# Layer 1's SSD in a two-layer hybrid backbone: decay differences and order of the projections rewritten

## The chip, the cores and the metric

The kernel runs on one core of one Trainium2 chip. The metric is the device time of one execution in microseconds (us), median over runs. Besides the DMA queues the core has five engines that each work through their own instructions in program order: PE (TensorE), DVE (VectorE), ACT (ScalarE), POOL (GpSimd) and SP (SyncE, which here issues the DMAs).

## The reference

The reference is a two-layer backbone over 512 latent and 256 context tokens of width 1024. Layer 0 mixes with MLA attention beside an RWKV-7 scan, layer 1 with a Mamba-2 SSD scan beside windowed grouped attention with a sink; behind each mixer stands a convolutional FFN. The change touches layer 1's mixer alone:

```python
def ssd_scan(x, dt, a_log, bm, cm, h0):          # chunks of 128 tokens, 2 groups x 8 heads, 64 channels a head
    a_cum = jnp.cumsum(dtc * a, axis=2)
    seg = a_cum[:, :, :, None] - a_cum[:, :, None, :]
    decay_qk = jnp.exp(jnp.where(tri[:, :, None, None], seg, -jnp.inf))
    cb = jnp.einsum('bcqgn,bckgn->bcqkg', cc, bc)
    y_diag = jnp.einsum('bcqkgh,bckghp->bcqghp', cb[..., None] * decay_qk * dtc[:, :, None], xc)
    ...                                           # chunk states, carried from chunk to chunk: h_in
    y_off = jnp.einsum('bcqgn,bcghpn,bcqgh->bcqghp', cc, h_in, jnp.exp(a_cum))
    return y_diag + y_off, h_last

def ssd_bidirectional(f_ctx, f_lat, p):           # the same scan forwards and backwards, with decays of their own
    ...
def swa_latent(q, k, v, k_ctx, v_ctx, sink):      # per block of 128 queries: softmax over context and window, times v
    ...
def mixer_ssd_swa(h_ctx, h_lat, p, rope, need_ctx):
    z, xbc, dt, q, k, v = split_cols(h @ p['w_in'], CD_SPLITS)
    ...
    out_l = jnp.concatenate([gated_rms_norm(y_l, z_l, g), att_l], axis=-1) @ p['w_out']
```

## The kernel before

Every large product is `dense` (L367): 8 slices of the inner dimension, each in three passes, weights high part by activations high part, low by high, high by low. A weight tile of 128 output rows is loaded as `wraw` (512 KB), cast to `whi` by ACT (L327), and `wlo` is the rest, by DVE or POOL (L328). Over 768 tokens a tile is 24 pairs of matmuls of 512 and 256 columns, over the 512 latent ones 24 of 512. All matmuls go through `mm`, so they carry line 269. PSUM is shared by name: `acc` (two tiles of 1024 columns), `sd` (three of 512), `b1`.

The code is written stage by stage, and a list scheduler with a model of the engines fixes each engine's order before the run. It may put later independent instructions ahead of earlier ones; buffers and semaphores then hold an engine that comes too soon. On the chip an engine never passes a waiting instruction.

Layer 1's mixer runs in these steps:

1. `decays()` projects `dt`, cumulates the decays of 48 rows (two directions of 16 heads, padded), writes them to DRAM as `sp_ac`, and makes `acm` (the cumulated decay by token), `wgt`, `dec` and `dtm`.
2. B and C of both groups (`bf`, `cf`, `btm`), then, for the eight tiles of x, four to a group: `dense`, a convolution of five taps on ACT and DVE (`conv5`, L1247 and L1251), and six transposes to `xtm`.
3. For each group: ten chunk states (POOL `xw`, a product into `sd`, DVE `hn`: L1342 to L1352), four products `cb` of B and C, and then four latent chunks c, each in two directions d. For one (c, d):
 - a DMA spreads 8 heads' cumulated decay over all partitions, `E` of 128x8x128 (512 KB);
 - ACT takes its exponential as `G` (L1373), POOL multiplies it by C (L1374);
 - DVE subtracts the token's own decay from `E` and cuts it at 0, one instruction a head (L1376), ACT takes the exponential (L1378), DVE multiplies by `dtm` and the masked `cb`, one instruction a head (L1381).

 PE then forms for each head and direction two products into the same bank, `hn` by `G` and `xtm` by `E`: 32 products of 64 rows by 128 columns a chunk. DVE adds the bank to `ym` (L1393).
4. Keys, values and four query tiles, with rope and splits that go to DRAM (`sl_k`, `sl_q0` to `sl_q3`); the rope buffers take over the room of `xtm0`.
5. Eight tiles of z gate `ym`; then the windowed attention, block by block (`swa_block`): for each block of keys and each of the two key groups, scores into `ab`, an exponential `pt`, and the value product `o<-pt,vv`, 64 rows by 512 columns, each group into its own half of the partitions. Tiles of the output projection (`wo`) are worked in between.

In this order group 0's chunks come between x tiles of group 1, keys, values and queries, and group 1's chunks among the z tiles.

Of the kernel before, what the change touches and what calls it, by code (L numbers as in the profile page):

```python
# [212 lines left out]
def hybrid_kernel(ctx: ExitStack, tc: tile.TileContext, a, out):  # L213
# [1110 lines left out]
    open_pool("sw", "right")  # L1324
    seq = ([0, 1, 2, 3, 4, 5], [1, 0, 5, 4, 3, 2])
    for g in range(2):
        for j in range(4 * g, 4 * g + 4):
# [7 lines left out]
            token_major(xtm[j // 4][:, :, (j % 4) * P:(j % 4 + 1) * P], o)  # L1335
        hin = {}
        for d in range(2):
            hprev = None
            hs = slice(32 * d + 8 * g, 32 * d + 8 * g + 8)
            for i, c in enumerate(seq[d][:-1]):  # L1340
                xw = T("sw", [P, 512], "xw", 2)
                ptt(out=xw.rearrange(h3, x=64), in0=xtm[g][:, c].rearrange(h3, x=64),  # L1342
# [21 lines left out]
        for c in range(2, 6):
            ls = slice((c - 2) * P, (c - 1) * P)
            E, G = [], []
            for d in range(2):
# [2 lines left out]
                dma(e.rearrange("p h t -> p (h t)"),  # L1370
                    acd[c, h0:h0 + 8].rearrange("h t -> (h t)").unsqueeze(0).partition_broadcast(P))
# [1 line left out]
                act(gc, e, AF.Exp)  # L1373
                ptt(out=gc, in0=gc, in1=cf[g][:, ls].unsqueeze(1).to_broadcast([P, 8, P]), op=ALU.mult)  # L1374
                for h in range(8):
                    ts(out=e[:, h], in0=e[:, h], scalar1=acm[:, c, h0 + h:h0 + h + 1], scalar2=0.0, op0=ALU.subtract,  # L1376
                       op1=ALU.min)
                act(e, e, AF.Exp)  # L1378
                cb = cbs[c, d]
                for h in range(8):  # L1380
                    stt(out=e[:, h], in0=e[:, h], scalar=dtm[:, c, h0 + h:h0 + h + 1], in1=cb, op0=ALU.mult,  # L1381
                        op1=ALU.mult)
# [13 lines left out]
    rq = T("sx", [P, 6, 512], "xtm0")  # L1396
    ropc, rops = rq[:, 0], rq[:, 1]
# [118 lines left out]
    def swa_block(i, es):  # L1516
# [5 lines left out]
        for n, tb in enumerate(tbs):  # L1522
# [125 lines left out]
```

## Time and profile before

| | before |
|---|---|
| median of 3 runs | 2253.11 us (2247.74 to 2253.65) |
| the profiled execution | 2259.24 us, of which 2257.2 us from the first to the last instruction |
| mean granted PE clock | 0.955 |
| PE busy | 2066.3 us, 92% |
| DVE, ACT, POOL busy | 1393.8, 930.8 and 506.2 us |
| HBM traffic | 125 GB/s over the span |

Busy times are those of one profiled execution. In the rows that follow, `acc<-h,whi` means: written tile, then what was read, with buffer numbers left out; `xN` is a count of instructions. A PE product of two plain fp32 operands shows as two instructions, one of the split kind (fp32r) as one. Matmuls overlap, so that their durations add up to more than the time that passes; the distance from one start to the next is the better measure. The granted clock is a share of the full PE clock.

### The profile page before, as it was taken

Reading aid. Unit: us, or ns where it says so; the run is one execution under the profiler, and the core shown is the slowest. Engines: PE = TensorE matmul, PEld = TensorE weight load, DVE = VectorE, ACT = ScalarE, POOL = GpSimd, SP = SyncE. Lnnn points to the kernel's source line nnn. Section 1 sums busy time; section 2 is a strip of 40 time slices with the busy share of each in tenths; the row PEclk is TensorE's granted clock in tenths of the full one; section 3 lists DMA queues with packets and bytes.
Section 4 is the critical chain, followed back from the end, with each engine's and each line's share of the span. In section 5 each row is a group of like instructions: output and inputs, shape, how many; then the busy total and the mean of one; then the engine's idle time right before and its main releaser. Section 6 shows DMA issues by size and latency. Waiting matters only on the chain.

```text
span 2257.2 us, 33584 instructions
## 1 busy us (share of the span) xinstructions
PE 2066.3 (92%) x13360; PEld 1636.3 (72%) x13360; DVE 1393.8 (62%) x2157; ACT 930.8 (41%) x1437; POOL 506.2 (22%) x486
## 2 busy tenths in 40 slices
PE   5888989788998999999999999898878999999997
PEld 3666667576654878888888886776665667888886
DVE  5566865666877466456465554678984556554555
ACT  4445663532355253233132335644353345332434
POOL 0027686521233100000000014433631330000000
PEclk9989999698999999999999999998999999999998
DMA  8477777669521443333233333213426032323231
GB/s 300 121 202 197 192 204 192 213 175 294 168 96 54 152 140 114 102 103 119 87 115 101 103 112 117 90 47 117 133 85 159 28 126 71 94 89 98 84 117 61
DMA packets 183660, 292.00 MB, mean 129 GB/s; under 512 B 63616, under 2 KB 118944, under 8 KB 180432
## 3 DMA queue, kind: packets, MB, share of 16 engines
q1 hardware_dynamic: 183504, 289.86, 41.8%
q8 instruction: 105, 1.72, 0.3%
q14 instruction: 51, 0.42, 0.1%
HBM read 234.87 MB, written 47.33 MB: 125 GB/s over the span
## 4 chain that ended last, share of the span: by engine, by line
PE 64%; DVE 7%; ACT 5%; DMA 4%; issue 3%; POOL 1%; SPq 1%; DVEq 0%; ACTq 0%; POOLq 0%
PE acc L269 50%; PE sd L269 3%; PE b L269 3%; PE o L269 2%; PE ab L269 2%; PE wo L269 2%; DVE E L1376 2%; DMA E<-sp_ac 1%; PE ax L269 1%; POOL I L767 1%; DMA rec<-sp_rec 1%; POOL w L765 1%; ACT L433 0%; PE iv L269 0%; PE gk L269 0%
## 5 line engine op out<-in xcount | busy, mean ns | idle before, releaser
L269 PE MATMUL acc<-s,whi 128*128 128x512 f32 (+1 forms) x3104 | 766.6, 358 | 1.6 <-ACT s L480 1.6
L269 PEld LDWEIGHTS acc<-s,whi 128*128 128x128 f32 x3104 | 546.2, 188 | 93.9 <-ACT s L480 5.5
L269 PE MATMUL acc<-s,wlo 128*128 128x512 f32 (+1 forms) x1552 | 456.4, 354 | 0.0
L269 PE MATMUL acc<-h,whi 128*128 128x256 f32 (+2 forms) x1248 | 318.9, 369 | 18.6 <-DVE f L385 8.0
L327 ACT CAST whi<-wraw 128x1024 fp32r<-128x1024 f32 (+5 forms) x228 | 210.2, 923 | 278.3 <-PE acc L269 202.9
L269 PEld LDWEIGHTS acc<-s,wlo 128*128 128x128 f32 x1552 | 289.9, 188 | 47.1 <-DVE wlo L328 0.7
L269 PEld LDWEIGHTS acc<-h,whi 128*128 128x128 f32 (+1 forms) x1248 | 221.0, 195 | 71.4 <-issue 15.2
L328 DVE TENSOR_TENSOR wlo<-wraw,whi 128x1024 fp32r<-128x1024 f32 (+5 forms) x205 | 218.6, 1070 | 45.6 <-ACT whi L327 45.0
L383 DVE SCALAR_TENSOR_TENSOR s<-acc,pv,s 128x511 f32<-128x511 f32 (+1 forms) x132 | 87.0, 659 | 204.4 <-ACT s L382 204.0
L382 ACT ACTIVATE s<-acc,pv 128x512 f32<-128x512 f32 (+1 forms) x132 | 93.3, 707 | 234.8 <-PE acc L269 198.9
L501 DVE SCALAR_TENSOR_TENSOR x<-acc,mods,x 128x512 f32<-128x512 f32 (+1 forms) x136 | 79.4, 620 | 172.2 <-PE acc L269 172.1
L269 PE MATMUL acc<-h,wlo 128*128 128x256 f32 (+2 forms) x624 | 178.4, 360 | 0.0
L451 POOL TENSOR_TENSOR f<-f,f 128x768 f32<-128x768 f32 (+1 forms) x24 | 31.4, 1308 | 632.9 <-ACT f L446 623.0
L269 PEld LDWEIGHTS acc<-h,wlo 128*128 128x128 f32 (+1 forms) x624 | 118.4, 193 | 21.8 <-issue 5.5
L1194 POOL TENSOR_TENSOR s<-w,s 128x256 f32<-128x256 f32 x6 | 5.0, 861 | 382.9 <-ACT s L433 382.9
L385 DVE SCALAR_TENSOR_TENSOR s<-acc,pv,s 128x511 f32<-128x511 f32 (+1 forms) x132 | 87.0, 659 | 3.7
L767 POOL TENSOR_TENSOR I<-I,w 128x30 f32<-128x30 f32 (+14 forms) x120 | 77.4, 645 | 9.0
L765 POOL TENSOR_TENSOR w<-I 128x30 f32<-128x30 f32 (+14 forms) x120 | 68.9, 574 | 34.9 <-PE iv L269 26.0
L328 POOL TENSOR_TENSOR wlo<-wraw,whi 128x1024 fp32r<-128x1024 f32 x23 | 62.9, 2735 | 58.1 <-ACT whi L327 54.6
L389 ACT CAST s<-s 128x768 fp32r<-128x768 f32 (+1 forms) x44 | 32.0, 728 | 106.0 <-DVE s L1164 105.9
L1376 DVE TENSOR_SCALAR E<-E,acm 128x128 f32<-128x128 f32 x128 | 61.2, 547 | 15.0 <-ACT G L1373 15.0
L740 DVE TENSOR_TENSOR W<-gk,con 64x512 f32<-64x512 f32 x48 | 32.8, 683 | 53.5 <-ACT PB L739 50.7
(389 smaller groups left out, 3390.1 us busy)
## 6 DMA issues: line engine op xcount, KB each, us to landing
wraw<-up SPq DMA_DIRECT2D x88, 512.0 KB, 3.5
aw<-ada SPq DMA_DIRECT2D x72, 512.0 KB, 5.7
rec<-sp_rec SPq DMA_DIRECT2D x24, 1024.0 KB, 7.5
wraw<-w_in SPq DMA_DIRECT2D x47, 512.0 KB, 3.6
aw<-ada1t SPq DMA_DIRECT2D x40, 512.0 KB, 4.3
wraw<-down SPq DMA_DIRECT2D x40, 384.0 KB, 3.2
sp_rec<-tg SPq DMA_DIRECT2D x24, 384.0 KB, 3.2
E<-sp_ac SPq DMA_DIRECT2D x16, 512.0 KB, 6.1
```

Of the source, the lines that this page charges most:

```text
L269: ins = nc.tensor.matmul(o, lhsT=lhsT, rhs=rhs, start=start, stop=stop, skip_group_check=shared)
L327: nc.scalar.copy(hi[:, :kt], raw[:, :kt])
L328: (eng or tt)(out=lo[:, :kt], in0=raw[:, :kt], in1=hi[:, :kt].bitcast(F32), op=ALU.subtract)
L382: act(o[rows, t0:t0 + n], ps[rows, po:po + n], AF.Identity, scale=w1, bias=b)
L383: stt(out=o[rows, t0 + 1:t0 + n], in0=ps[rows, po:po + n - 1], scalar=w0, in1=o[rows, t0 + 1:t0 + n], op0=ALU.mult, op1=ALU.add)
L385: stt(out=o[rows, t0:t0 + n - 1], in0=ps[rows, po + 1:po + n], scalar=w2, in1=o[rows, t0:t0 + n - 1], op0=ALU.mult, op1=ALU.add)
L389: nc.scalar.copy(hi, src)
L501: stt(out=x[:, t0:t0 + n], in0=ps[:, po:po + n], scalar=mods[:, c6 * 8 + m, c:c + 1], in1=x[:, t0:t0 + n], op0=ALU.mult, op1=ALU.add)
L740: tt(out=w[hk], in0=b[hk].rearrange("p c (a t) -> p c a t", a=2), in1=mk[hk].rearrange("p (a t) -> p a t", a=2).unsqueeze(1).to_broadcast( ...
L765: eng.tensor_tensor(out=tmp, in0=I[:, m + 1:, m:m + 1].to_broadcast([P, n, m]), in1=I[:, m:m + 1, :m].to_broadcast([P, n, m]), op=ALU.mult)
L767: eng.tensor_tensor(out=I[:, m + 1:, :m], in0=I[:, m + 1:, :m], in1=tmp, op=ALU.add)
L1376: ts(out=e[:, h], in0=e[:, h], scalar1=acm[:, c, h0 + h:h0 + h + 1], scalar2=0.0, op0=ALU.subtract, op1=ALU.min)
```

## The change

- `decays()` also splits the cumulated decay into a high and a low part and writes both to DRAM (`sp_acp`).
- A constant `sel` (512 KB, loaded twice) is cast into `rq0` and `rq1`; `lk0` and `lk1` start as ones. For each (c, d) two DMAs of one partition (8x128) put the chunk's decays into `rq`, and `lk` holds the decays by token.
- PE forms the decay differences: for each half of the heads one product of `rq` by `lk`, and one of `idr` (the identity) by `drop`, which adds a large negative number where the mask is to cut. ACT takes the exponential from PSUM as `E`, and DVE multiplies it by `cb` in one instruction for all eight heads. The masked `cb` and the eight subtractions and eight multiplications a (c, d) are gone.
- The inter-chunk part is `hin` by C (`cf`), four products of 128x128 a (c, d) into `sd`. DVE multiplies them by `eg`, the exponential of the cumulated decay, which two DMAs of 64x4x128 bring (128 KB each) in a pair of buffers. `G` is gone.
- `dtm` moves from `E` to x: POOL makes `xd` (in the buffers `xw`, three instead of two).
- The value products of a chunk are 16 instead of 32; DVE adds the two `eg` and then both parts to `ym`.
- The order in the code is now: all eight x tiles, the chunks of group 0, keys, values and queries, the chunks of group 1, z.
- In `swa_block` the value product of group 1 is issued first, and that of group 0 right behind it.

```diff
@@ decays
+        parts = tc.dram_tile([2, 48, NTOK], F32, name="sp_acp")
+        phi, plo = F(F32R), F(F32R)
+        nc.scalar.copy(phi[H48], ac[H48])
+        tt(out=plo[H48], in0=ac[H48], in1=phi[H48].bitcast(F32), op=ALU.subtract)
+        for x, t in enumerate((phi, plo)):
+            dma(parts[x], t[H48].bitcast(F32))
@@ ahead of the x tiles
+    idr = T("sw", [P, P], "idr", 1, F32R)
+    nc.scalar.copy(idr, ident)
...
+        ts(out=m, in0=ge if d else le, scalar1=-1.0, scalar2=1e30, op0=ALU.add, op1=ALU.mult)
+        drop.append(m)
+    rq = [T("sw", [P, 8, P], f"rq{d}", 1, F32R) for d in range(2)]
+    lk = [T("sw", [P, NLAT], f"lk{d}", 1, F32R) for d in range(2)]
+    for d in range(2):
+        raw = T("sw", [P, 8, P], "E", 3)
+        dma(raw.rearrange("p h t -> p (h t)"), a["sel"])
+        nc.scalar.copy(rq[d], raw)
+        nc.vector.memset(lk[d].bitcast(F32), 1.0)
@@ chunks, now a function ssd(g)
+        for d in range(2):
+            for x in range(2):
+                dma(lk[d][8 * x:8 * x + 8].bitcast(F32), parts[x, 32 * d + 8 * g:32 * d + 8 * g + 8, L0:L1])
...
-                e = T("sw", [P, 8, P], "E", 4)
-                dma(e.rearrange("p h t -> p (h t)"),
-                    acd[c, h0:h0 + 8].rearrange("h t -> (h t)").unsqueeze(0).partition_broadcast(P))
-                gc = T("sw", [P, 8, P], "G", 4)
-                act(gc, e, AF.Exp)
-                ptt(out=gc, in0=gc, in1=cf[g][:, ls].unsqueeze(1).to_broadcast([P, 8, P]), op=ALU.mult)
-                for h in range(8):
-                    ts(out=e[:, h], in0=e[:, h], scalar1=acm[:, c, h0 + h:h0 + h + 1], scalar2=0.0, op0=ALU.subtract,
-                       op1=ALU.min)
-                act(e, e, AF.Exp)
-                cb = cbs[c, d]
-                for h in range(8):
-                    stt(out=e[:, h], in0=e[:, h], scalar=dtm[:, c, h0 + h:h0 + h + 1], in1=cb, op0=ALU.mult,
-                        op1=ALU.mult)
+                for x in range(2):
+                    dma(rq[d][16 + x:17 + x].bitcast(F32), parts[x, h0:h0 + 8, c * P:(c + 1) * P].unsqueeze(0))
+                eg = T("sw", [P, 4, P], "eg", 2)
+                for par in range(2):
+                    dma(eg[H[par]], acd[c, h0 + par:h0 + 8:2].unsqueeze(0).partition_broadcast(64))
+                act(eg, eg, AF.Exp)
+                ps = acc()
+                for x in range(2):
+                    px = ps[:, x * 512:x * 512 + 512]
+                    mm(px, lhsT=lk[d][:, ls], rhs=rq[d][:, 4 * x:4 * x + 4]..., start=True, stop=False)
+                    mm(px..., lhsT=idr, rhs=drop[d]..., start=False, stop=True)
+                e = T("sw", [P, 8, P], "E", 3)
+                act(e.rearrange("p h t -> p (h t)"), ps, AF.Exp)
+                tt(out=e, in0=e, in1=cbs[c].unsqueeze(1).to_broadcast([P, 8, P]), op=ALU.mult)
+                xd = T("sw", [P, 512], "xw", 3)
+                ptt(out=xd..., in0=xtm[g][:, c]..., in1=dtm[:, c, h0:h0 + 8]..., op=ALU.mult)
+                z = sdbank()
+                for j in range(4):
+                    mm(z[:, j * P:(j + 1) * P], lhsT=hin[d, c][:, j * P:(j + 1) * P], rhs=cf[g][:, ls], start=True, stop=True)
+                tt(out=eg, in0=z.rearrange(v4, b=P), in1=eg, op=ALU.mult)
...
                 for d in range(2):
-                    mm(o, lhsT=hin[d, c][:, hx], rhs=G[d][:, h], start=d == 0, stop=False)
-                    mm(o, lhsT=xtm[g][:, c, hx], rhs=E[d][:, h], start=False, stop=d == 1)
+                    mm(o, lhsT=X[d][:, hx], rhs=E[d][:, h], start=d == 0, stop=d == 1)
             yo = ym[g][:, :, ls]
+            tt(out=Z[0], in0=Z[0], in1=Z[1], op=ALU.add)
+            tt(out=yo, in0=yo, in1=Z[0], op=ALU.add)
             tt(out=yo, in0=b.rearrange(v4, b=P), in1=yo, op=ALU.add)
+    ssd(0)
 ...
+    ssd(1)
@@ swa_block
-            for g in range(2):
-                mm(o[H[g]], lhsT=vv[:, tb * P + 64 * g:tb * P + 64 * g + 64], rhs=pts[g], start=n == 0,
-                   stop=n == len(tbs) - 1)
+            for g in (1, 0):
+                with tc.issue_after(pe_last[0]) if g == 0 else nullcontext():
+                    mm(o[H[g]], lhsT=vv[:, tb * P + 64 * g:tb * P + 64 * g + 64], rhs=pts[g], start=n == 0,
+                       stop=n == len(tbs) - 1)
```

How the instructions move is told by the order on the engines. On PE before, a product of group 0's fourth chunk (`sd_13275`) stands in the middle of a dense tile (`acc_14095`, one of the tiles behind x):

```order
L269 MATMUL acc_14095<-h_12125,wlo_13547 128x256
L269 MATMUL acc_14095<-h_12125,wlo_13547 128x512
L269 MATMUL sd_13275<-G_13233,hn_12937 64x128
L269 MATMUL acc_14095<-h_12163,whi_13546 128x256
L269 MATMUL acc_14095<-h_12163,whi_13546 128x512
L269 MATMUL acc_14095<-h_12130,whi_13546 128x256
```

Now PE's row behind the last x tile holds small products only: decay differences (`acc<-rq,lk` and `acc<-drop,idr`), the products `cb` (`sd<-cf,bf`), `hin` by C (`sd<-cf,hn`), then values:

```order
L273 MATMUL sd_13317<-cf_12555,bf_12431 128x128 x4
L273 MATMUL acc_13422<-rq_1752_12610,lk_1754_12612 128x512
L273 MATMUL acc_13422<-drop_1750_12607,idr_12603 128x512
L273 MATMUL acc_13422<-rq_1752_12610,lk_1754_12612 128x512
L273 MATMUL acc_13422<-drop_1750_12607,idr_12603 128x512
L273 MATMUL sd_13346<-cf_12555,hn_13257 128x128 x4
```

The first dense row after them is one of the tile of keys, within the third chunk; the rest of that tile goes on into the fourth. Among group 1's chunks stand 48 of the 192 products of z.

On DVE before, in group 0's third and fourth chunk, with convolution steps (L1251) between them:

```order
L1376 TENSOR_SCALAR E_13175<-E_13175,acm_12335 128x128 x8
L1381 SCALAR_TENSOR_TENSOR E_13153<-E_13153,dtm_12334,cb_12989 128x128 x8
L1251 SCALAR_TENSOR_TENSOR f_13598<-acc_13543,pv_71,f_13598 128x511
L1376 TENSOR_SCALAR E_13231<-E_13231,acm_12335 128x128 x8
L1381 SCALAR_TENSOR_TENSOR E_13175<-E_13175,dtm_12334,cb_12991 128x128 x8
```

DVE now, at group 1's first chunks (`E` times `cb`, `eg` times its product, the state `hn`, the sums into `ym`):

```order
L1415 TENSOR_TENSOR E_14009<-E_14009,cb_13990 128x1024
L1415 TENSOR_TENSOR E_14031<-E_14031,cb_13990 128x1024
L1415 TENSOR_TENSOR E_14073<-E_14073,cb_13992 128x1024
L1422 TENSOR_TENSOR eg_14000<-sd_14014,eg_14000 128x512
L1383 TENSOR_TENSOR hn_13980<-sd_13981,hn_13980 128x512
L1422 TENSOR_TENSOR eg_14022<-sd_14036,eg_14022 128x512
L1433 TENSOR_TENSOR eg_14000<-eg_14000,eg_14022 128x512
L1434 TENSOR_TENSOR ym_1698_12247<-ym_1698_12247,eg_14000 128x4x128
```

Sixteen instructions a (c, d) became two, one sum a chunk became three, and no convolution step lies between.

On PE in the windowed attention before, the value products of the two key groups stand apart:

```order
L269 MATMUL o_14939<-pt_14962,vv_14412 64x512
L269 MATMUL ab_14982<-qa_14376,ka_14372 128x512
L269 MATMUL ab_14982<-qb_14378,kb_14374 128x512
L269 MATMUL ab_14982<-mle_14363,identr_14360 128x512
L269 MATMUL o_14939<-pt_14971,vv_14412 64x512
L269 MATMUL ab_14988<-qa_14377,ka_14373 128x512
```

Now they stand in a row:

```order
L273 MATMUL wo_15327<-go_14741,wlo_14632 128x512
L273 MATMUL o_14844<-pt_14867,vv_14317 64x512
L273 MATMUL o_14844<-pt_14862,vv_14317 64x512
L273 MATMUL ab_14887<-qa_14281,ka_14277 128x512
L273 MATMUL ab_14887<-qb_14283,kb_14279 128x512
```

Of the 18 pairs 4 stood in a row before, and 17 do now.

More of the change, by code (lines that the diff above doesn't have):

```diff
@@ L206, in layout @@
     a["scan2"] = cs["scan2"]
+    sel = np.zeros((P, 8, P), np.float32)
+    for h in range(8):
+        sel[h, h], sel[8 + h, h] = -1.0, -1.0
+    a["sel"] = sel.reshape(P, 8 * P)
     a["const1"] = np.concatenate([cs["le"], cs["ge"]], 1)
@@ L1300, in decays @@
         act(dec, dec, AF.Exp)
-        return acm, wgt, dec, dtm, acd
+        return acm, wgt, dec, dtm, acd, parts
     if DTJ < 0:
-        acm, wgt, dec, dtm, acd = decays()
+        acm, wgt, dec, dtm, acd, parts = decays()
     bf, cf, btm = [], [], []
@@ L1325, in hybrid_kernel @@
     seq = ([0, 1, 2, 3, 4, 5], [1, 0, 5, 4, 3, 2])
+    idr = T("sw", [P, P], "idr", 1, F32R)
+    nc.scalar.copy(idr, ident)
+    drop = []
+    for d in range(2):
+        m = T("sw", [P, P], f"drop{d}", 1, F32R)
+        ts(out=m, in0=ge if d else le, scalar1=-1.0, scalar2=1e30, op0=ALU.add, op1=ALU.mult)
[7 more added lines that the diff above has]
+        nc.vector.memset(lk[d].bitcast(F32), 1.0)
     for g in range(2):
@@ L1328, in hybrid_kernel @@
             if j == DTJ:
-                acm, wgt, dec, dtm, acd = decays()
+                acm, wgt, dec, dtm, acd, parts = decays()
             ps = acc()
@@ L1335, in hybrid_kernel, with ssd @@
             token_major(xtm[j // 4][:, :, (j % 4) * P:(j % 4 + 1) * P], o)
+    def ssd(g):
+        for d in range(2):
+            for x in range(2):
+                dma(lk[d][8 * x:8 * x + 8].bitcast(F32), parts[x, 32 * d + 8 * g:32 * d + 8 * g + 8, L0:L1])
         hin = {}
@@ L1340, in hybrid_kernel @@
             for i, c in enumerate(seq[d][:-1]):
-                xw = T("sw", [P, 512], "xw", 2)
+                xw = T("sw", [P, 512], "xw", 3)
                 ptt(out=xw.rearrange(h3, x=64), in0=xtm[g][:, c].rearrange(h3, x=64),
@@ L1360, in hybrid_kernel @@
         for c in range(2, 6):
-            for d in range(2):
-                cbs[c, d] = T("sw", [P, P], "cb", 8)
-                tt(out=cbs[c, d], in0=b[:, (c - 2) * P:(c - 1) * P], in1=ge if d else le, op=ALU.mult)
+            cbs[c] = T("sw", [P, P], "cb", 4)
+            nc.vector.tensor_copy(cbs[c], b[:, (c - 2) * P:(c - 1) * P])
         for c in range(2, 6):
             ls = slice((c - 2) * P, (c - 1) * P)
-            E, G = [], []
+            E, X, Z = [], [], []
             for d in range(2):
@@ new lines, in ssd @@
+                act(eg, eg, AF.Exp)
+                ps = acc()
+                for x in range(2):
+                    px = ps[:, x * 512:x * 512 + 512]
+                    mm(px, lhsT=lk[d][:, ls], rhs=rq[d][:, 4 * x:4 * x + 4].rearrange("p h t -> p (h t)"), start=True,
+                       stop=False)
+                    mm(px.rearrange(v4, b=P), lhsT=idr, rhs=drop[d].unsqueeze(1).to_broadcast([P, 4, P]),
+                       start=False, stop=True)
+                e = T("sw", [P, 8, P], "E", 3)
@@ new lines, in ssd @@
+                act(e.rearrange("p h t -> p (h t)"), ps, AF.Exp)
+                tt(out=e, in0=e, in1=cbs[c].unsqueeze(1).to_broadcast([P, 8, P]), op=ALU.mult)
+                xd = T("sw", [P, 512], "xw", 3)
+                ptt(out=xd.rearrange(h3, x=64), in0=xtm[g][:, c].rearrange(h3, x=64),
+                    in1=dtm[:, c, h0:h0 + 8].unsqueeze(2).to_broadcast([P, 8, 64]), op=ALU.mult)
+                z = sdbank()
+                for j in range(4):
+                    mm(z[:, j * P:(j + 1) * P], lhsT=hin[d, c][:, j * P:(j + 1) * P], rhs=cf[g][:, ls], start=True, stop=True)
@@ L1383, in hybrid_kernel @@
+                tt(out=eg, in0=z.rearrange(v4, b=P), in1=eg, op=ALU.mult)
+                Z.append(eg)
+                X.append(xd)
                 E.append(e)
-                G.append(gc)
             b = sdbank()
@@ L1389, in hybrid_kernel @@
                 for d in range(2):
[L1390 to L1391 removed]
+                    mm(o, lhsT=X[d][:, hx], rhs=E[d][:, h], start=d == 0, stop=d == 1)
             yo = ym[g][:, :, ls]
+            tt(out=Z[0], in0=Z[0], in1=Z[1], op=ALU.add)
+            tt(out=yo, in0=yo, in1=Z[0], op=ALU.add)
             tt(out=yo, in0=b.rearrange(v4, b=P), in1=yo, op=ALU.add)
+    ssd(0)
     lat = {}
[L1396 to L1397 removed]
+    rp = T("sx", [P, 6, 512], "xtm0")
+    ropc, rops = rp[:, 0], rp[:, 1]
     dma(ropc, a["rope_c"])
@@ L1401, in rope64 @@
     def rope64(o, i):
-        w = rq[:, 2 + i % 2]
+        w = rp[:, 2 + i % 2]
         for r in range(4):
@@ L1421, in hybrid_kernel @@
     rope64(o[:, L0:], 0)
-    spill_split("k", o, rq[:, 4:].rearrange("p a b -> p (a b)")[:, :NTOK].bitcast(F32R), NTOK)
+    spill_split("k", o, rp[:, 4:].rearrange("p a b -> p (a b)")[:, :NTOK].bitcast(F32R), NTOK)
     ps = acc()
@@ L1435, in hybrid_kernel @@
         rope64(o, j + 1)
-        spill_split(f"q{j}", o, rq[:, 4 + j % 2].bitcast(F32R), NLAT)
+        spill_split(f"q{j}", o, rp[:, 4 + j % 2].bitcast(F32R), NLAT)
+    ssd(1)
     close_pool("sw", "sx")
```

## The prediction

> **What bounds the kernel now.** I read the page first (busy shares, the chain that ended last), then the busy time by stretch of layer 1's mixer, then its waits, its groups of instructions, and the timeline of PE.
>
> ```profile
> span 2257.2 us, 33584 instructions
> PE 2066.3 (92%) x13360; PEld 1636.3 (72%) x13360; DVE 1393.8 (62%) x2157; ACT 930.8 (41%) x1437; POOL 506.2 (22%) x486
> ...
> PE 64%; DVE 7%; ACT 5%; DMA 4%; issue 3%; POOL 1%; SPq 1%; DVEq 0%; ACTq 0%; POOLq 0%
> ```
>
> PE is busy for 92% and the chain lies on it. What can be gained is idle PE, a lower clock, or PE work. The stretches (columns after the length: PE, PEld, DVE, ACT and POOL busy, granted clock, DMA) show where the idle part lies:
>
> ```profile
> 1440.00:1530.00 90.00, 89.50 (x570) 74.61 (x569) 65.56 (x127) 41.96 (x64) 40.58 (x23) 1.00 0.17 55
> 1530.00:1550.00 20.00, 11.68 (x65) 9.62 (x62) 17.16 (x34) 9.61 (x10) 9.59 (x4) 0.74 0.29 98
> ...
> 1640.00:1700.00 60.00, 44.35 (x280) 35.00 (x277) 43.17 (x87) 28.91 (x33) 17.84 (x7) 0.93 0.40 103
> ...
> 1740.00:1820.00 80.00, 80.00 (x314) 47.64 (x314) 41.16 (x60) 29.22 (x56) 25.89 (x20) 1.00 0.14 43
> sum 420.00, PE 370.68 PEld 277.76 DVE 294.47 ACT 186.36 POOL 157.77; mean PE 41.19 PEld 30.86 DVE 32.72 ACT 20.71 POOL 17.53
> ```
>
> Of 420 us from 1400 to 1820 PE idles 49.3; the x tiles (1440 to 1530) and the windowed attention (1740 to 1820) hold next to none of it, the chunks with keys, queries and z nearly all. What PE waits for there, and what its helpers wait for:
>
> ```profile
> POOL G L1374 <- ACT G L1373: 61.9, 7, 23.2
> ...
> ACT E L1378 <- DVE E L1376: 40.4, 12, 6.9
> ```
>
> The chain from `E` over DVE, ACT and DVE again to PE is late. The start of the x tiles and the longest gap behind it, on PE (in brackets the idle time and what ended it), and what DVE did in that gap and elsewhere:
>
> ```profile
> 1431.75 0.90 PE L1260 MATMUL b<-con,f 128*128 128x128 f32 x3 [8.44 <-ACT f L1254]
> ...
> 1544.14 0.69 PE L269 MATMUL sd<-E,xtm 128*64 128x128 f32 x2 [8.32 <-DVE E L1381]
> ```
>
> ```profile
> 1425.21 1.65 DVE L1376 TENSOR_SCALAR E<-E,acm 128x128 f32<-128x128 f32 x8
> 1532.84 6.00 DVE L1376 TENSOR_SCALAR E<-E,acm 128x128 f32<-128x128 f32 x8 [3.46 <-ACT G L1373]
> ```
>
> The same eight subtractions take 1.65 us at 1425 and 6.00 at 1533. The Trainium skill (GPSIMD Engine Reference, Architecture) says that POOL shares its SBUF port with DVE; what I take here from the two rows is only the spread.
>
> **The change, part by part.** Durations are those of the stretch 1400 to 1705, by form:
>
> ```profile
> L1376 DVE TENSOR_SCALAR E<-E,acm 128x128 f32<-128x128 f32 x128 | 61.2, 547 | 15.0 <-ACT G L1373 15.0
> L1374 POOL TENSOR_TENSOR G<-G,cf 128x1024 f32<-128x1024 f32 x16 | 40.0, 2515 | 62.2 <-ACT G L1373 61.9 <-ACT cf L1254 0.3
> L1381 DVE SCALAR_TENSOR_TENSOR E<-E,dtm,cb 128x128 f32<-128x128 f32 x128 | 34.7, 343 | 0.0
> L1342 POOL TENSOR_TENSOR xw<-xtm,wgt 128x512 f32<-128x512 f32 x20 | 23.5, 1189 | 8.0 <-PE sd L269 7.4 <-ACT xtm L1261 0.6
> L1350 DVE TENSOR_TENSOR hn<-hn,dec 128x512 f32<-128x512 f32 x16 | 16.5, 1032 | 1.5 <-ACT hn L1348 1.3
> L1352 DVE TENSOR_TENSOR hn<-sd,hn 128x512 f32<-128x512 f32 x16 | 10.9, 683 | 1.4 <-PE sd L269 0.8
> L328 DVE TENSOR_TENSOR wlo<-wraw,whi 128x1024 fp32r<-128x1024 f32 x6 | 7.3, 1217 | 0.6 <-ACT whi L327 0.5
> L1411 ACT CAST xtm<-f 128x512 fp32r<-128x512 f32 x4 | 2.5, 620 | 19.6 <-DVE f L1407 10.9 <-issue 8.7
> ```
>
> *DVE.* Gone: 61.2 + 34.7 (and eight of the masked `cb`, not counted). New: 16 `E` times `cb` of 128x1024, priced by `wlo` (1.22 each, 19.5); 16 `eg` times its bank and 16 more sums, priced by the `hn` sum (.68 each, 21.8); about 2 for split and masks. Net 95.9 less 43.3: 53 us fewer. POOL: 40.0 of `G` against 16 `xd` at 1.19, 19.0. ACT: 16 exponentials of `G` become 16 of half the width, near .62 by the cast of that shape; two casts into `rq` come in. None of these engines bounds by its sum: they matter as chains.
>
> *PE.* Prices are distances between starts:
>
> ```profile
> 1524.65 0.44 PE L269 MATMUL sd<-G,hn 128*64 128x128 f32 x4
> ...
> 1525.14 0.44 PE L269 MATMUL sd<-G,hn 128*64 128x128 f32 x4
> ```
>
> ```profile
> 1513.04 1.02 PE L269 MATMUL sd<-xw,btm 128*128 128x512 f32 x2
> 1513.90 1.05 PE L269 MATMUL sd<-cf,bf 128*128 128x128 f32 x8
> 1514.71 0.47 PE L269 MATMUL acc<-h,wlo 128*128 128x512 f32 x1
> ...
> 1730.74 0.39 PE L269 MATMUL wo<-go,whi 128*128 128x512 f32 x1
> 1730.97 0.39 PE L269 MATMUL wo<-go,wlo 128*128 128x512 f32 x1
> ```
>
> Four products of 64 rows take .49 (1524.65 to 1525.14): a chunk's 32 took 3.9 us, its 16 take 2.0. Four of 128x128 take .81 (1513.90 to 1514.71), a state .86, one fp32r product of 512 columns .23. So a chunk has now 2.0 + 1.6 (`hin` by C) + 1.9 (eight for the decays) = 5.5 us against 3.9: the change *adds* 13 us of PE work over eight chunks. It must pay by the idle time and the clock.
>
> *Stage by stage.* The x tiles start at 1432 as before, behind ACT's and DVE's convolutions of B and C: no gain, 3 us either way as bounds, since four `E` loads less lie in front and two casts more. A tile over 768 tokens is 24 x .23 x 1.5 = 8.3, eight are 66, eight of ten states of group 0 among them 7; with 8 for transposes and hand-overs the last ends at 1513. Then group 0: until the first values DVE has two states (1.03 + .68 each) and three `E` products (1.22 each), 7 us, behind the last x tile's convolution; group 1's start, with all its states, comes to 21 below. Between 7 and 21 I take 16, since the last convolution and its transposes stand ahead: 1529. From then on a chunk goes round: four `eg` issues on SP (.37 each, as `E`'s), landing, exponential .62, `eg` times bank .68, two sums 1.4, and the buffer is free. For the issue there is `E`'s row (ns, shortest, median, longest), for the landing the rows differ (KB, median us):
>
> ```profile
> L1370 SPq DMA_DIRECT2D E<-sp_ac x16: 320/372/2253, 1414.0 to 1643.1; - x16
> ...
> E<-sp_ac SPq DMA_DIRECT2D x16, 512.0 KB, 6.1
> ...
> xtm<-f SPq DMA_DIRECT2D x20, 64.0 KB, 2.5
> qa<-sl_q0hi SPq DMA_DIRECT2D x4, 128.0 KB, 6.0
> qa<-sl_q1hi SPq DMA_DIRECT2D x4, 128.0 KB, 5.1
> ```
>
> `qa` has `eg`'s very shape, but 24 such loads are issued in a row there; four at a time stand nearer to the 2.5 of `xtm`. With 2.5 a round takes 7 us, with 5.1 about 9.5; I take 8. The tile of keys (8.3 us of PE) lies inside. So the tile of values begins 3 x 8 + 2 = 26 us behind 1529, at 1555. It and four query tiles (24 products of 512 columns each) are 8.3 + 96 x .23 = 30, with transposes 31: 1586. Group 1 starts with all ten states: DVE has 8 x 1.71 + 3.7 + 1.4 = 19 us, 21 with the first product and its hand-overs; three rounds and a tail are 26, 48 of the 192 z products among them: 1633. The other 144 are 33: 1666. The stretch ends, as before, with loads of `qa` that PE waits for:
>
> ```profile
> 1697.16 0.36 PE L269 MATMUL sd<-ka,qa 128*128 128x256 f32 x1 [1.96 <-DMA qa<-sl_q0hi]
> ...
> 1700.96 0.58 PE L269 MATMUL sd<-ka,qa 128*128 128x256 f32 x1 [3.22 <-DMA qa<-sl_q1hi]
> ```
>
> With the same 5 us, and 2 for what else is in the row, the attention starts at 1673 instead of 1701: 28 us earlier. What loses its cover is the chain itself: dense work used to run while DVE made `E`, now a slow chain stops PE at once.
>
> *Value products.* In the attention PE is never idle (80.00 of 80), so a saving there counts in full:
>
> ```profile
> 1734.53 1.08 PE L269 MATMUL o<-pt,vv 128*64 128x512 f32 x4
> 1735.54 0.50 PE L269 MATMUL ab<-qa,ka 128*128 128x512 f32 x1
> ...
> 1736.21 1.07 PE L269 MATMUL o<-pt,vv 128*64 128x512 f32 x2
> 1737.21 0.50 PE L269 MATMUL ab<-qa,ka 128*128 128x512 f32 x1
> ```
>
> Two products in a row (x4) take 1.01 us, one alone (x2) 1.00: the halves run side by side. 13 pairs close up: 13 us; since a pair now waits for the later of two exponentials I take 12 (8 to 13).
>
> *Ahead of the x tiles.* `sel` and the casts into `rq` fall on ACT in front of the short norm chain: +1 (0 to 6, if `sel` lands as late as `E`). The two writes of `sp_acp` and 32 `rq` loads of 4 KB and 32 of `eg`, less 16 of `E`, add about 50 issues on SP at .37, 19 us over a stretch of 300: hidden behind rounds of 8, but in front of the weight loads.
>
> Sum: -28 - 12 + 1 = -39 us. Each link was taken free of the next one's delays, so I take -35: 2259 becomes 2224 for a profiled execution, and the median, which lies 6 us below it, 2218.
>
> **The rivals.** (1) *The `eg` round is the bound.* At 9.5 us a round, with `qa`'s landing, six rounds on the path cost 9 more, and group 0 delays queries by SP's queue; with four more for that the gain is 22: 2231. For it: `qa` at 5.1 to 6.0. Against: 512 KB a chunk now, 1 MB before.
>
> (2) *The bare chain is slower than the covered one* and the kernel loses. `E` times `cb` on DVE would stretch like the subtractions did (6.00 against 1.65) under POOL's `xd` and `wlo`: 2 x 1.22 become up to 2 x 4.4, and with a landing of 5.1 behind it a round takes 9.5 + 6.4 = 16. Six rounds at 8 more are 48, less the 35: 2266. It decides from 14 us a round on. Against it: POOL has 21 us less to do, and DVE 53.
>
> (3) *The clock drops in the bare stages.* It was .74 in the 20 us around the gap of 8.32. If group 0's and group 1's stages (42 and 47 us, some 75 us of PE work) ran at .74, they would take 26 us more, of which I count 60% on the path: gain 19, 2234. Against it: a round of 8 us has 5.5 of PE work, so no gap is near 8 us. The Trainium skill (TensorE: Matmul & The Clock Gate, What's actually happening) puts the clock at half after an idle window of about 3.4 us; by an estimate from that page the 75 us would double in the worst case and the gain would be gone. The row's .74 is a mean over 20 us, which a half clock for part of it fits, but a gap of 2.5 us does not reach the page's window.
>
> (4) *Only the value products count*: PE's added 13 us and new waits eat what the chunks gain; 12 us faster, 2241.
>
> **How the numbers follow.** Chances: my forecast .47, (1) .18, (3) .10, (4) .07, no change (both parts even out) .07, (2) .11. Two runs of this kernel differ by up to .3%, 7 us, which is what a measurement can tell. Faster .82, same .07, slower .11. The likeliest case alone spans 2203 (rounds of 7, 13 from the values, no delay by `sel`, x tiles 3 us earlier: 50 in all) to 2230; the range reaches over (1), (3) and (4) to no change: 2200 to 2252.
>
> **What would show it.** Right: PE idle in the stretch between the x tiles and the attention falls from 49 us to about 25, groups for `E` times `cb` at 1.2 to 1.6 us, z's last dense product near 1671, value products as x4 about 1.0 apart. Wrong: `eg` landing above 5 us with DVE waiting for ACT's `eg`; PE waiting for DVE's `E` product over 5 us at a time; a granted clock below .8 in the chunks; the x tiles starting after 1436.

## The result, and the profile after

The changed kernel takes 2237.98 us (median of 6 runs, 2233.57 to 2242.91), the kernel before 2253.38 us beside it (6 runs). The ratio is 0.9933, 95% interval 0.9915 to 0.9951: about 15 us faster, where 35 were forecast. The time lies above the 2203 to 2230 of the likeliest case, though still inside the whole range of 2200 to 2252, which reached to no change at all. The page of the profile after, same parts as before (span, busy shares, the chain by engine):

```profile
span 2236.6 us, 33363 instructions
PE 2058.3 (92%) x13296; PEld 1641.9 (73%) x13296; DVE 1355.8 (61%) x1946; ACT 921.4 (41%) x1438; POOL 482.7 (22%) x486
...
PE 66%; DVE 8%; ACT 4%; DMA 4%; issue 2%; POOL 1%; SPq 1%; DVEq 0%; ACTq 0%; POOLq 0%
```

DVE lost 38 us over the whole program, POOL 24, and PE is as busy as before. Layer 1's mixer by stage, after (columns as in the prediction: length, PE, PEld, DVE, ACT, POOL busy, clock, DMA share, GB/s):

```profile
1504.80:1551.60 46.80, 41.60 (x292) 32.19 (x290) 36.49 (x48) 22.81 (x30) 14.00 (x12) 0.93 0.20 60
1551.60:1585.00 33.40, 33.40 (x162) 27.82 (x162) 12.70 (x12) 11.46 (x16) 11.86 (x7) 1.00 0.52 162
1585.00:1617.30 32.30, 21.62 (x66) 12.88 (x64) 28.08 (x32) 7.12 (x10) 18.91 (x14) 0.79 0.26 91
1617.30:1648.70 31.40, 30.02 (x233) 24.66 (x232) 21.61 (x24) 11.78 (x16) 7.68 (x6) 0.94 0.39 118
1648.70:1702.30 53.60, 46.03 (x186) 36.65 (x185) 26.29 (x37) 21.58 (x28) 9.84 (x4) 0.87 0.57 158
1702.30:1718.50 16.20, 13.20 (x54) 10.50 (x52) 11.90 (x20) 12.91 (x23) 0.00 (x0) 0.79 0.11 32
1718.50:1816.00 97.50, 97.43 (x430) 62.84 (x429) 56.81 (x70) 42.76 (x83) 38.21 (x26) 1.00 0.13 42
```

In order of the rows: group 0's chunks with keys, then values and queries, group 1's start up to its first value products, group 1's chunks, z with the attention's first row maxima, the rest of the attention's lead, and the attention from its first value product to its last. That last stage took 109.5 us before:

```profile
1734.50:1844.00 109.50, 108.94 (x464) 65.70 (x463) 54.92 (x76) 43.68 (x86) 36.91 (x29) 1.00 0.17 56
```

PE is full in both, and the stage is 12.0 us shorter. The two stages don't hold the same work besides the value products (tiles of the output projection moved), so the pairs' own gain is better read from the distances between starts: those of `o<-pt,vv` add up to 19.6 us now and to 31.5 before. The value products now follow each other in pairs (x4), in the same 1.0 us that one of them took:

```profile
1718.54 1.08 PE L273 MATMUL o<-pt,vv 128*64 128x512 f32 x4
1719.55 0.50 PE L273 MATMUL ab<-qa,ka 128*128 128x512 f32 x1
```

The third row of the stages is where the forecast breaks first: 32.3 us from the last query to group 1's first value products, with PE busy for 21.6 of them at a clock of .79. PE waits there for the states:

```profile
1595.57 2.05 PE L273 MATMUL sd<-xw,btm 128*128 128x512 f32 x2 [5.04 <-DVE hn L1383]
...
1615.32 2.08 PE L273 MATMUL sd<-cf,hn 128*128 128x128 f32 x8 [5.11 <-DVE hn L1383]
```

and DVE works on the last queries' rope and split (L1449, L1450, L1455) in front of and between the states' steps (L1381, L1383), in its fixed order:

```profile
1587.63 1.53 DVE L1449 TENSOR_TENSOR f<-f,xtm 128x512 f32<-128x512 f32 x1
1589.27 2.66 DVE L1450 TENSOR_TENSOR f<-f,xtm 128x512 f32<-128x512 f32 x1
1591.85 1.52 DVE L1381 TENSOR_TENSOR hn<-hn,dec 128x512 f32<-128x512 f32 x1
1593.30 1.53 DVE L1455 TENSOR_TENSOR f<-f,xtm 128x512 fp32r<-128x512 f32 x1
1594.74 0.68 DVE L1383 TENSOR_TENSOR hn<-sd,hn 128x512 f32<-128x512 f32 x1
```

### The profile page after: what moved, and what is told of

Its sections match the earlier page's. It is cut to its first block, busy times and chain, and to the rows that moved or that the text cites. A ratio compares the mean times of both kernels' runs of the same rounds, so it can differ in the third digit from the quotient of the medians.

```text
span 2236.6 us, 33363 instructions
## 1 busy us (share of the span) xinstructions
PE 2058.3 (92%) x13296; PEld 1641.9 (73%) x13296; DVE 1355.8 (61%) x1946; ACT 921.4 (41%) x1438; POOL 482.7 (22%) x486
## 4 chain that ended last, share of the span: by engine, by line
PE 66%; DVE 8%; ACT 4%; DMA 4%; issue 2%; POOL 1%; SPq 1%; DVEq 0%; ACTq 0%; POOLq 0%
PE acc L273 52%; PE sd L273 3%; PE b L273 3%; PE wo L273 2%; PE ab L273 2%; PE o L273 2%; DVE f L1255 1%; DMA wraw<-w_out 1%; PE ax L273 1%; POOL I L771 1%; POOL w L769 1%; DMA rec<-sp_rec 1%; DMA eg<-sp_ac 0%; DVE hn L1381 0%; PE iv L273 0%
## 5 line engine op out<-in xcount | busy, mean ns | idle before, releaser
L273 PE MATMUL acc<-h,whi 128*128 128x256 f32 (+2 forms) x1248 | 311.0, 363 | 21.7 <-DVE f L1255 6.1
L332 POOL TENSOR_TENSOR wlo<-wraw,whi 128x1024 fp32r<-128x1024 f32 x23 | 56.4, 2453 | 100.7 <-ACT whi L331 100.4
L1255 DVE SCALAR_TENSOR_TENSOR f<-acc,pv,f 128x254 f32<-128x254 f32 (+3 forms) x80 | 48.4, 613 | 29.5 <-ACT f L1251 28.1
L273 PE MATMUL bkp<-aw,sc 128*32 128x256 f32 x384 | 35.8, 457 | 30.7 <-DMA aw<-ada 28.8
```

What stands on the lines that cost most here:

```text
L273: ins = nc.tensor.matmul(o, lhsT=lhsT, rhs=rhs, start=start, stop=stop, skip_group_check=shared)
L332: (eng or tt)(out=lo[:, :kt], in0=raw[:, :kt], in1=hi[:, :kt].bitcast(F32), op=ALU.subtract)
L1255: stt(out=o[:, t0 + lo:t0 + hi], in0=ps[:, po + lo + s:po + hi + s], scalar=col(f"sconv_w{tap}", j), in1=o[:, t0 + lo:t0 + hi], op0=ALU.mu ...
```

## The experiments

Two theories at the outset. A: nearly all of the gain is the value products', and the chunks brought next to nothing, because new waits took the place of the old. B: the chunks gained, and the pairs only shifted work. Ratios are to the kernel before, run beside each, with 95% intervals.

| run | median us | ratio (95%) |
|---|---|---|
| changed kernel | 2237.98 | 0.9933 (0.9915 to 0.9951) |
| e1 pairs alone | 2240.93 | 0.9944 (0.9929 to 0.9958) |
| e2 all but the pairs | 2251.9 | 0.9997 (0.9985 to 1.0009) |
| e3 new chunks, old order | 2273.95 | 1.0080 (1.0066 to 1.0094) |
| e4 old chunks, new order | 2263.23 | 1.0043 (1.0030 to 1.0057) |
| e5 states early | 2221.94 | 0.9860 (0.9845 to 0.9874) |
| e6 e5, E in four buffers | 2223.58 | 0.9862 (0.9849 to 0.9876) |
| e7 e5, eg in four buffers | 2228.62 | 0.9883 (0.9868 to 0.9899) |
| e8 mask product twice | 2236.25 | 0.9916 (0.9903 to 0.9930) |
| e9 e5, chunks before queries | 2240.32 | 0.9944 (0.9930 to 0.9958) |
| e10 e5, xw in five buffers | 2222.09 | 0.9860 (0.9843 to 0.9877) |
| e11 e5, maxima between z tiles | 2222.61 | 0.9855 (0.9838 to 0.9872) |
| e12 e5 without the pairs | 2238.7 | 0.9930 (0.9912 to 0.9947) |
| e13 e5, mask product twice | 2222.12 | 0.9859 (0.9845 to 0.9873) |
| e14 e5, a quarter of hin by C | 2216.38 | 0.9843 (0.9824 to 0.9861) |

**e1, e2: the two halves of the change.** e1 is the kernel before with

```diff
-            for g in range(2):
-                mm(o[H[g]], lhsT=vv..., rhs=pts[g], ...)
+            for g in (1, 0):
+                with tc.issue_after(pe_last[0]) if g == 0 else nullcontext():
+                    mm(o[H[g]], lhsT=vv..., rhs=pts[g], ...)
```

and e2 is the changed kernel with that part undone.

> The kernel before with the closed-up value products alone (group 1 first, group 0 right behind). Theory A (nearly all of the 15 us come from the pairs; in the changed kernel the distances of o<-pt,vv add up to 19.6 us against 31.5): 12 us faster than before, about 2241, ratio .994 to .996. Theory B (the chunks bring most, the pairs only shift work of wo behind the attention): within 4 us of before, 2249 to 2253.

> The changed kernel with the value products in the order of before. Theory A: 3 us faster than before (2250, within 1 to 6). Theory B: 11 us or more faster than before (2242 or less).

e1 is 12.4 us faster than before, e2 is the same as before (1.5 us, within its interval). Theory A holds and B falls: the pairs are worth what the prediction gave them, and all else together brings nothing to the time. (That does not mean that nothing else moved: see the stretches under "Why the prediction was wrong".)

**e4, e3: chunks and order apart.** e4 takes the new order of the code with the old chunks, e3 the new chunks (and the pairs) in the old order:

```diff
 e4, from before:
+    def ssd(g):
         hin = {}
 ...
+    ssd(0)
     lat = {}                  # keys, values, queries
 ...
+    ssd(1)
     close_pool("sw", "sx")
 e3, from the changed kernel:
             token_major(xtm[j // 4]..., o)
+        ssd(g)
-    ssd(0)
 ...
-    ssd(1)
```

> The kernel before with the code order of the change alone: all x tiles, group 0's chunks with G and the per-head subtractions, keys, values, queries, group 1's chunks, z. If the order is what eats the gain of the new chunks (bare starts of both groups), it is slower than before, by 10 to 30 us, since the old chain of DVE is longer by 53 us and stands bare. If the order is neutral or a gain by itself: within 5 us of before, or faster.

> The changed kernel, value pairs included, with the chunks written where they stood before: behind the fourth x tile for group 0, behind the eighth for group 1, ahead of keys. The old mathematics lost 10 us by the new order (and 22 against the pairs' 2241 once the pairs are taken out on both sides is 10). If the new mathematics gains by itself and the new order takes it back: about 2228 (10 faster than the changed kernel). If the new mathematics brings nothing by itself (13 us more PE work for the waits it saves) and the order suits it: 2241 or slower.

The order alone costs the old chunks 10 us; the new chunks in the old order are 34 us slower than in the new one (each against the kernel before beside it), against both readings that I had offered (2228 or 2241). So neither part has a price of its own: the new chunks need the new order, and the new order alone loses. In e3 the stages from group 1's start on, and the wait for the attention's loads behind z (PE, stage by stage), are:

```profile
1560.00:1598.00 38.00, 23.57 (x76) 11.87 (x74) 22.84 (x33) 12.40 (x17) 16.47 (x13) 0.92 0.05 16
...
1675.00:1700.00 25.00, 13.20 (x49) 10.05 (x48) 10.70 (x13) 7.44 (x11) 6.09 (x3) 0.75 0.67 154
```

In e4 the attention's loads are late, too: with group 1's chunks last, PE stands for 12 us in front of the first scores.

```profile
1702.99 0.55 PE L269 MATMUL sd<-ka,qa 128*128 128x256 f32 x1 [12.07 <-DMA qa<-sl_q0hi]
```

**e5, e12: group 1's start.** The ten states of group 1 are issued right behind group 0's chunks, so that they run among the tiles of values and queries:

```diff
-    ssd(0)
+    states(0)
+    chunks(0)
+    states(1)
 ...  # keys, values, queries
-    ssd(1)
+    chunks(1)
```

> The changed kernel with group 1's ten states issued ahead of keys and queries, so that they run among those dense tiles; group 1's chunks stay where they are. Theory A's reading (group 1's start took 32 us with 11 idle at a clock of .79, for the states' chain behind the last query's rope and split on DVE): 7 to 12 us faster than the changed kernel, about 2229. Rival (the start is bound by the loads of eg and rq and the rounds, not by the states): within 3 us of the changed kernel, 2235 to 2241.

> Group 1's states early, value products in the order of before. If the pairs' 12 us and the states' 16 add up: 2234, 12 us slower than 2222, so that the new chunks with the states early are worth 19 us by themselves. If the pairs only pay where the attention is otherwise full of waits, or the earlier states change what the pairs bring: 2228 or less.

e5 gains 16 us on the changed kernel, more than expected, and is 31 us faster than before. Its start of group 1 (first row) is 9 us instead of 32, while the chunks behind it take as long as they did; PE now waits once, for the first products of `E` and `cb`:

```profile
1598.00:1607.00 9.00, 4.52 (x32) 3.99 (x31) 8.21 (x12) 4.51 (x6) 4.18 (x3) 0.96 0.57 203
1607.00:1638.00 31.00, 29.60 (x223) 23.70 (x223) 24.43 (x28) 11.70 (x15) 8.06 (x6) 0.90 0.43 134
```

```profile
1607.04 0.66 PE L273 MATMUL sd<-E,xw 128*64 128x128 f32 x2 [4.51 <-DVE E L1418]
```

Not all of the 23 us saved in that stage show, since the states' own PE work (10 x .86) went into the stages before. Without the pairs (e12) the same kernel is 15.8 us faster than before: that is what the new chunks in the new order are worth once the states are covered, against 1.5 in e2. The pairs then bring about 16 instead of 12; the intervals allow 11 to 21. Part of this may not be the pairs: without them, in e2 as in e12, one more tile of the output projection (24 products of `wo`) stands behind the last value product.

**e6, e10, e7: are the rounds of a chunk bound by a buffer?** Each is e5 with one pool made larger.

```diff
 e6:  -  e = T("sw", [P, 8, P], "E", 3)      +  e = T("sw", [P, 8, P], "E", 4)
 e10: -  xw = T("sw", [P, 512], "xw", 3)     +  xw = T("sw", [P, 512], "xw", 5)
 e7:  -  eg = T("sw", [P, 4, P], "eg", 2)    +  eg = T("sw", [P, 4, P], "eg", 4)
```

> Group 1's states early (as in the run before) and four buffers for E instead of three. If the rounds of a chunk (8.1 us in group 0 of the changed kernel) are set by E's buffers, which wait for the last values: rounds near 6 to 7, 3 to 8 us faster than with three, about 2216. If by eg or the dense tiles between them: within 2 us of 2222.

> Group 1's states early and five buffers for xw and xd instead of three. POOL waits 52 us for PE to free one in the changed kernel (1500 to 1710), the longest wait there. If that wait is on the path of the rounds: 3 to 6 us faster than 2222. If it is only POOL's own slack: within 2 us of 2222.

> Group 1's states early and four buffers for eg instead of two. Rival 1 of the prediction (the eg round is the bound): rounds shorten, 4 us or more faster than 2222. If E and the values set the round: within 2 us of 2222.

None is faster. In the changed kernel POOL waited 52.1 us for room in `xw` and ACT 40.6 us for `eg`, by far the longest waits of these stages (groups of 1500 to 1660; the last columns are the idle time ahead and what ended it):

```profile
L1415 DVE TENSOR_TENSOR E<-E,cb 128x1024 f32<-128x1024 f32 x16 | 20.7, 1332 | 1.0 <-ACT E L1414 1.0
...
L1417 POOL TENSOR_TENSOR xw<-xtm,dtm 128x512 f32<-128x512 f32 x16 | 18.5, 1173 | 52.1 <-PE sd L273 52.1
...
L1422 DVE TENSOR_TENSOR eg<-sd,eg 128x512 f32<-128x512 f32 x16 | 10.8, 686 | 11.2 <-ACT eg L1404 6.9 <-PE sd L273 4.3
...
L1404 ACT ACTIVATE eg<-eg 128x512 f32<-128x512 f32 x14 | 8.8, 631 | 41.4 <-DMA eg<-sp_ac 40.6 <-DVE eg L1422 0.8
```

and more room there buys nothing: they were these engines' slack. e7 is even some 5 us slower than e5 (the intervals touch). In its trace an `eg` exponential comes earlier, into ACT's row in front of C's activation, with a table load on each side of it, and PE waits 5 us ahead of an x tile:

```profile
1436.69 1.28 ACT L1407 ACT_TABLE_LOAD   x1
1437.98 0.63 ACT L1407 ACTIVATE eg<-eg 128x512 f32<-128x512 f32 x1
1438.63 1.28 ACT L1258 ACT_TABLE_LOAD   x1
```

```profile
1440.97 0.90 PE L1264 MATMUL b<-con,f 128*128 128x128 f32 x3 [5.19 <-ACT btm L1265]
```

But this is not where the 5 us went. Counted from the norm's first product ahead of the mixer, e7's first value product comes after 339.1 us and e5's after 338.2, so the delay has been made up by then. The loss stands behind the last value product, where e7 has one tile of `wo` more than e5 and takes 430.1 us to the end instead of 422.1.

**e8, e13, e14: did the added PE work eat the gain?** e8 is the changed kernel and e13 is e5 with the mask product issued twice; e14 is e5 with three quarters of the inter-chunk products left out.

```diff
 e8, e13:
+                    for again in range(2):
                         mm(px..., lhsT=idr, rhs=drop[d]..., start=False, stop=again == 1)
 e14:
-                for j in range(4):
+                for j in range(1):
                     mm(z[:, j * P:(j + 1) * P], lhsT=hin[d, c]..., rhs=cf[g][:, ls], start=True, stop=True)
-                tt(out=eg, in0=z.rearrange(v4, b=P), in1=eg, op=ALU.mult)
+                tt(out=eg, in0=z[:, :P].unsqueeze(1).to_broadcast([P, 4, P]), in1=eg, op=ALU.mult)
```

> The changed kernel with the product of idr by drop issued twice (the sum under the mask is -2e30 instead of -1e30, the exponential 0 either way): 32 products of .23 us, 7.4 us more on PE. If the added PE work of the change counts in full: 7 us slower than the changed kernel, 2245. If it lies in PE's waits: within 2 us, 2236 to 2240.

> Group 1's states early, and the product of idr by drop issued twice: 32 products of .23 us, 7.4 us more on PE. If PE work in the chunks counts in full once group 1's start no longer waits: 7 us slower than states early alone, 2229. If it lies in waits of the chunks' chain: within 2 us of 2222.

> Group 1's states early, and of the four products hin by C of each chunk and direction only the first, which stands for all four (this leaves out three quarters of the inter-chunk part): 48 products of .20 us, 9.7 us less on PE. If the 13 us of PE work that the change adds are what is left of the shortfall: 8 to 10 us faster than states early alone, 2213. If the chunks' chain sets the pace: within 2 us of 2222.

7.4 us more on PE cost nothing in either kernel; 9.7 us less bring about 4, with an interval that reaches from none to 9. So the 13 us that the change adds are not the bulk of what is missing. e13 is the cleaner of the two additions, since in e8 a tile of `wo` moved behind the attention as well. From the norm's first product to the first value product PE idles for 31.3 us in e5 and for 26.9 in e13, within the same 338 us: 4.4 of the 7.4 us went into idle time. Group 0's stage shows where the rest can have gone: the clock is higher there. Here e5, then e13, 50 us from the same point of the program:

```profile
1504.00:1554.00 50.00, 44.80 (x310) 35.07 (x310) 38.79 (x52) 23.14 (x30) 14.57 (x12) 0.93 0.18 56
```

```profile
1498.00:1548.00 50.00, 46.40 (x330) 36.81 (x329) 40.51 (x52) 23.76 (x31) 15.70 (x14) 1.00 0.22 67
```

e8 has 1.00 there, too, against .93 in the changed kernel. But e6, with no product added, has .97, so that the work alone is not shown to be the cause: the order and the length of the waits changed with it.

**e9, e11: the way into the attention.** e9 is e5 with group 1's chunks ahead of the queries, e11 is e5 with the first block's row maxima behind four z tiles:

```diff
 e9:   spill("v1", t)
+      chunks(1)
       for j in range(4):        # queries
 ...
-      chunks(1)
 e11: -    nxt = swa_max(0)
 ...   for g in range(2):        # z tiles
+          if g == 1:
+              nxt = swa_max(0)
```

> Group 1's states early and its four chunks ahead of the queries, so that query tiles instead of z tiles stand between them, and z follows the last query without a chunk in it. If it is the place of group 1's chunks right ahead of the attention's loads that keeps the last 9 us from showing: 4 to 9 us faster than states early alone (2222), about 2216. If the chunks only need dense tiles beside them, whichever: within 3 us of 2222. If rope and split of the queries, which now come last on DVE and POOL, delay the attention: slower, 2225 to 2232.

> Group 1's states early, and the first block's row maxima (scores sd<-ka,qa and their masks) written behind four of the eight z tiles instead of ahead of them. In the changed kernel the stretch from group 1's last chunk to the first value product took 70 us for 47 us of PE work, with PE waiting for loads of qa and for DVE's maxima inside z. If those waits are on the path because the maxima come too early: 3 to 7 us faster than 2222. If the first value product then waits for the maxima, or z's end sets everything: within 2 us, or slower.

e9 loses 18 us against e5, more than the worst reading gave. The queries' rope, split and stores now come last, so that PE waits for `qa` and then for the maxima. (The first value product comes 13.7 us later than in e5; another 6.3 stand behind the last one, where a tile of `wo` more is left; the attention itself is 4.9 shorter.)

```profile
1653.62 0.55 PE L273 MATMUL sd<-ka,qa 128*128 128x256 f32 x1 [6.28 <-DMA qa<-sl_q0hi]
...
1670.06 1.01 PE L273 MATMUL sd<-ka,qa 128*128 128x256 f32 x3 [3.77 <-DVE nc L1540]
```

So group 1's chunks between queries and attention are themselves a cover, for the queries' way through DRAM. e11 changes nothing.

## Why the prediction was wrong

The sum was -28 for the chunks and their order, -12 for the value products, +1 ahead of the x tiles, and 4 us of reserve.

- **Value products, -12: right.** e1 measured 12.4, and the distances fell by 11.9, with PE full before and after.
- **Ahead of the x tiles, +1: no loss.** The two casts of `rq` (1.0 each) lie in waits of ACT. Counted from the norm's first product, the x tiles start 1.9 us earlier than before (60.4 instead of 62.3 us), within the 3 either way.
- **Chunks and order, -28: this step failed.** It measured 1.5 (e2). Its links, by the traces' stages:
  - Group 0, rounds of 8, keys between them: right. Values start 126 us behind the first x tile, 123 were forecast; the rounds were 8.1. (An `eg` issue took .62, median of 32, where .37 was put in.)
  - Values and queries took 33.4, where 31 were forecast.
  - *Group 1's start, 21 us: it took 32.3.* I had counted DVE's steps for the states alone, 19 us, as if DVE and POOL began them free. They begin behind the last queries' rope and split, which stood on the same two engines, each state waits for the one before, and the clock fell to .79. I wrote that the chain "loses its cover", and then priced it only by its own durations. e5 shows this link's worth: 16 us when the states are covered.
  - *Group 1's rounds and tail, 26 us: 31.4*, and 31.0 in e5. I had priced a round at 8 by the chain of `eg`, and put 48 z products in for nothing. By the prediction's own prices PE's work in such a round is 5.5 for the chunk and 16 x .23 for z, 9.2 in all. PE is busy for 30.0 of the 31.4 us.
  - *From the last chunk to the attention.* I added z's 33 us and 5 of waits, and took the rest of the attention's lead as it stood before. It is no fixed piece. In that lead 68 products of `wo` ran before the first value product; now it is 12, and products of z lie between the maxima instead. Without `wo` the stretch from the last chunk to the first value product takes 67 us (69.8 less 12 x .23), where my terms come to 58 (73.5 less 68 x .23). PE waits there for `qa` and for DVE's maxima, at a clock of .87:

```profile
1665.27 0.35 PE L273 MATMUL sd<-ka,qa 128*128 128x256 f32 x1 [3.29 <-DMA qa<-sl_q0hi]
1682.40 0.46 PE L273 MATMUL sd<-ka,qa 128*128 128x256 f32 x1 [2.93 <-DVE nw L1544]
```

  These links add up to 11 + 5 + 9 + 5 (group 0 and queries) = 30, with the 56 products of `wo` that left the lead charged in full, and the -28 are gone.
- **PE work, +13.** The products were priced well, but their weight was not: e8 and e13 show that adding such work costs nothing in the end, and in e14 taking 9.7 us of it away brings about 4.
- **The rivals.** (1), the `eg` round, falls with e7. (2), a bare chain, came in part: not the rounds, as I had written it, but a start without cover, at 11 us beyond the sum. (3), the clock, is seen where PE waits (.79 and .87), not in the chunks themselves (.93 and .94). (4), "only the value products count" at 2241 with a chance of .07, is what came. Of its two reasons the new waits are borne out, PE's added work is not. Too much of the chance lay on the sum of links that each assumed the one before it on time.

Group 1's start is shown by e5 and e12. The rest can be counted in another way, by where it shows, and the traces then place it behind the attention. Here are the lengths in us of one execution each, from the norm's first product ahead of the mixer (PE's `acc<-f,ones`, at 1370.0 before):

| stretch | before | changed | e2 | e5 | e12 |
|---|---|---|---|---|---|
| to the first value product | 364.5 | 353.2 | 347.6 | 338.2 | 335.4 |
| from there to the last one | 108.7 | 96.7 | 105.4 | 95.3 | 103.1 |
| from there to the end | 414.0 | 421.4 | 430.7 | 422.1 | 430.5 |
| `wo` products in that last stretch | 24 | 96 | 120 | 96 | 120 |

The two last stretches before, then in the changed kernel, with two thirds of those products (`sh` by `go`; another third is `sl` by `go`):

```profile
1843.20:2257.20 414.00, 398.39 (x1910) 323.63 (x1908) 228.80 (x328) 161.20 (x236) 11.61 (x15) 0.98 0.29 92
L269 PE MATMUL wo<-sh,go x16: 278/283/386, 1843.9 to 1847.5; 128*128 128x256 f32 x16
```

```profile
1815.20:2236.60 421.40, 405.93 (x1984) 333.48 (x1980) 235.64 (x339) 165.25 (x245) 14.81 (x18) 0.98 0.30 97
L273 PE MATMUL wo<-sh,go x64: 280/283/386, 1816.0 to 1833.8; 128*128 128x256 f32 x64
```

In e5 the first value product comes 26.3 us earlier than before and the attention is 13.4 shorter, close to the sum's 27 and 12. Yet the tiles of the output projection that filled the lead before push others behind the last value product, and from there to the end it takes 8.1 longer. In the changed kernel it is 11.3 and 12.0 gained and 7.4 lost, 15.9 in all, where the medians give 15.4. So the sum was also wrong in taking it that an earlier attention ends the program earlier by as much: the dense work that leaves the lead has to be done behind it. No run moved `wo` alone, so this second price is read from the traces and not shown by an experiment. Neither larger buffers (e6, e7, e10) nor a later place of the maxima (e11) won it back; what another place of `wo` would bring stays open.

The best version that was run is e5 (the changed kernel with group 1's states early): 2221.94 us, ratio 0.986. e6, e10, e11 and e13 equal it.

What rival (3) took from the Trainium skill shows in group 1's start. Behind the wait of 5.04 us PE's products of 512 columns stand .43 apart (the last two rows), against .24 ahead of it:

```profile
1588.35 0.40 PE L273 MATMUL acc<-drop,idr 128*128 128x512 f32 x1
1588.59 0.39 PE L273 MATMUL acc<-rq,lk 128*128 128x512 f32 x1
...
1598.70 0.63 PE L273 MATMUL acc<-drop,idr 128*128 128x512 f32 x1
1599.13 0.63 PE L273 MATMUL acc<-rq,lk 128*128 128x512 f32 x1
```

The Trainium skill (TensorE: Matmul & The Clock Gate, What's actually happening) has half the clock after an idle window of about 3.4 us, and these rows agree with it, near enough to a half (.24 over .43 is .56).

## What to carry to other kernels

When a chain is moved off its cover, price its start by what stands ahead of it on the same in-order engines, not by its own durations: here 21 us became 32, and issuing the first links of the chain a stage earlier, among dense tiles, gave back 16. And follow the dense work that is pushed out of a stretch to where it lands: here tiles that left the attention's lead stood behind the attention, and the traces lose 7 to 8 us there. Two small products into opposite halves of the partitions cost one when they are neighbours in PE's row, and twice that when other products stand between; in a stage with PE full that was the whole gain of this change. A longest wait in a table is a question, not a cost: room for the two longest waits here bought nothing.

## What the runs showed of the hardware that was not expected

- More PE work can leave the time as it is and go with a higher granted clock: .93 and 1.00 over 50 us with 7 us of products added to the program (e5 and e13, and likewise the changed kernel and e8), one trace each. That the work is the cause is not shown.
- Moving one exponential on ACT into a stretch of another function brings two table loads of 1.28 us with it (e7); there the time was made up before the attention.
